# Regrouping the side work of a two-layer trunk: attention steps in groups, two transposed row tiles in one bank, state reads next to outer products

## The chip, the cores and the metric

The kernel runs on one core of a Trainium2 chip. The metric is the device time of one launch in microseconds; three runs are given for the kernel before, and their median is what a change is held against.

## The reference, cut to what matters

Two layers; each projects 512 tokens of 2048 features with one wide matrix, runs two kinds of heads on the result, and projects back. Around it stand RMS norms, SiLU gates and the residual sum.

```python
# softmax heads (8 of width 128): every frame sees its own chunk and the 8 before it
scores = einsum('bnqhd,bnkhd->bnhqk', qc, kb) * D ** -0.5 + bias
p = softmax(where(valid, scores, -inf)); o = einsum('bnhqk,bnkhd->bnqhd', p, vb)
# linear heads (4, keys 128, values 256), chunks of 64 frames
U = einsum('bnchk,bnchv->bnhkv', k * exp(L_end - L), v)      # outer products
state = exp(L_end) * state + U                               # one step per chunk
o = einsum('bnchk,bnhkv->bnchv', q * DK ** -0.5, states)     # reads
```

With 512 frames the band covers all earlier chunks, so each tile of 128 rows attends to the row tiles up to itself.

## The kernel before, in words

The bulk of the work is a list of large products: the projections, done as `std_gemm` (line 293) and, for the other pairs of column blocks, as `fast_gemm` (line 324), which forms seven products per pair out of sums of blocks. Each weight chunk is a Job: a load, a cast `wh` on ScalarE (line 201) and a remainder `wl` on VectorE (line 210), and then 12 matmuls of 512 columns (line 388), or 24 of 256 columns in the pairs that come out feature-major (line 378). A pair has 28 jobs. These matmuls take their operands as fp32r.

Everything else is side work. It is written as generators in `tasks` and is emitted between jobs: after each job `pace()` calls `pump(n)` (line 257), and each pump resumes the first generator of `tasks` up to its next `yield`. `delayed` holds calls that come due after so many pumps. `until` (line 272) pumps until a condition holds. The rate is 2.1 pumps a job in the pairs that hold the softmax heads, 2 in the pair that makes the linear heads' values (GV), and 3 in the pair after it (GG). This gives the program's order; the framework then simulates a timeline and lays out each engine's instructions by it, so that an instruction that is not ready in that simulation lets a later one go first, and the engines then run the order that came out.

Softmax attention: `attend` (line 988) runs two heads, a and b, through the hand-written list ORDER (line 983). `aS3` is the scores of row tile 3 of head a (`scores`, line 901: three fp32r matmuls, a DVE reduction at line 912, an exponential at 916). `aT3` transposes the probabilities of that tile (`trans`, line 924: i + 1 transposes of fp32 into one PSUM bank, then one copy out, by ScalarE for tiles 1 and 3 and by VectorE for 0 and 2). `aP3` multiplies them with the values (`mix`, line 935: i + 1 fp32 matmuls, each of which shows as two records, then a square on ScalarE). `aG` scales and gates the head (line 953), and eight pumps later `turn` (line 964) transposes its result. Each step ends in one `yield`, so a pair of heads takes 28 pumps.

Linear attention: `gla_heads` (line 1243) takes two heads in two halves each, four Units. `outer` (line 1089) forms a unit's chunk states' increments: 12 fp32r matmuls of 64 rows by 128 columns into two banks. `states` (line 1108) chains them on VectorE, four instructions. `read` (line 1124) multiplies queries with states: four fp32 matmuls of 128 rows by 64 columns, eight records. `norm` and `evict` follow on ScalarE, VectorE and GpSimd. Two of these generators run in each layer. A unit's reads are emitted six pumps after its states, five for the last unit; the outer product of unit k + 1 is emitted two pumps before the reads of unit k.

All side work takes its PSUM from one tag of four banks (`aux`, line 87).

Of the kernel before, what the change touches and what calls it, by code (L numbers as in the profile page):

```python
# [15 lines left out]
P = 128  # L16
L = 2
S = 512
# [15 lines left out]
def hybrid_trunk(  # L34
# [13 lines left out]
    nc = tc.nc  # L48
# [16 lines left out]
    def nm(s):  # L65
        serial[0] += 1
        return f"{s}_{serial[0]}"

    def slot(tag, shape, dtype=F32):
        return slots.tile([P] + shape, dtype, tag=tag, name=nm(tag))  # L70
# [4 lines left out]
    def t2(shape=(512,), dtype=F32):  # L75
        return tmp.tile([P] + list(shape), dtype, tag="t2", name=nm("t2"))
# [10 lines left out]
    def aux():  # L87
        return ps_ax.tile([P, 512], F32, tag="ax", name=nm("ax"))
# [12 lines left out]
    def flat(t):  # L101
        return t.bitcast(F32).rearrange("p a b -> p (a b)")

    def split(hi, lo, src):
        nc.scalar.copy(hi, src)
        return nc.vector.tensor_tensor(out=lo, in0=src, in1=hi.bitcast(F32), op=ALU.subtract).ins
# [9 lines left out]
    ident = cst[:, 0:P]  # L116
# [137 lines left out]
    delayed = []  # L254
# [356 lines left out]
    rows = []  # L611
# [117 lines left out]
    def layer(l):  # L729
# [163 lines left out]
        class Head:  # L893
# [28 lines left out]
                    load_bias(HEADS.index(self.hd) + 2)  # L922

            def trans(self, i):
                lk = (i + 1) * P
                ps = aux()
                for j in range(i + 1):
                    nc.tensor.transpose(ps[:, j * P : (j + 1) * P], self.prob[i][:, j * P : (j + 1) * P], ident)  # L928
                pt = self.pt[i] = t2((lk,))
                if i % 2:  # L930
                    nc.scalar.copy(pt, ps[:, :lk])
                else:
                    nc.vector.tensor_copy(pt, ps[:, :lk])
# [30 lines left out]
            def turn(self):  # L964
                c, kk = self.hd // 2, self.hd % 2
                if kk == 0:
                    turned[c] = slot("g16", [2, 512], F32R)
                ps = aux()
                for t in range(NT):
                    nc.tensor.transpose(ps[:, t * P : (t + 1) * P], self.sg[:, t, :], ident)  # L970
                kt = 8 + self.hd
                f = t2()
                nc.scalar.activation(
                    f, ps, AF.Copy, scale=gcol[:, l * 2 * KT + KT + kt : l * 2 * KT + KT + kt + 1]
                )
                last_turn[0] = nc.gpsimd.dma_start(of_att[l][c][:, kk, :], f).ins
                ks = slice(kk * 256, (kk + 1) * 256)
                z = turned[c]
                split(z[:, 0, ks], z[:, 1, ks], f[:, 0:256])
                if kk:  # L980
                    nc.gpsimd.dma_start(oa_d[l][c], flat(z))

        ORDER = (
            "aS3 aS2 aS1 aS0 aT3 bS3 aT2 aP3 bS2 aT1 aP2 bS1 aT0 aP1 bS0 aP0 - aG "
            "bT3 bT2 bP3 bT1 bP2 bT0 bP1 bP0 - bG"
        ).split()

        def attend(hd, qk):
            heads = {"a": Head(hd, qk, 0), "b": Head(hd + 1, qk, 1)}

            def turn(h):
                h.turn()
                if h.hd % 2:
                    heads_done.add(hd)

            for _ in range(5 if hd == HEADS[0] else 0):
                yield
            for step in ORDER:
                if step == "-":
                    yield  # L1000
                    continue
                h = heads[step[0]]
                if step[1] == "S":
                    h.scores(int(step[2]))
                elif step[1] == "T":
                    h.trans(int(step[2]))
                elif step[1] == "P":
                    h.mix(int(step[2]))
                else:
                    h.gate()  # L1010
                    delayed.append([8, lambda h=h: turn(h)])
                yield

        QKT = {(0, 1): ("g4", "g5", "g6", "g7"), (0, 0): ("g8", "g9", "g10", "g11"),
# [2 lines left out]
        def qk_consume(p):  # L1017
            sets = {}

            def f(j, h, b, src, comb):  # L1020
                if j not in sets:
                    if (p, j) == (1, 0):
                        until(lambda: 2 in heads_done)
                    sets[j] = [slot(tag, [2, 512], F32R) for tag in QKT[p, j]]
                z = settled(src, comb).rearrange("p (f n) -> p f n", f=2)
                hs = slice(h * 256, (h + 1) * 256)
                hi, lo = sets[j][2 * b][:, :, hs], sets[j][2 * b + 1][:, :, hs]
                if b == 0:
                    split_scaled(hi, lo, z, -QS)
                else:  # L1030
                    split(hi, lo, z)
                if h and b:
                    tasks.append(attend(4 * p + 2 * j, sets[j]))
            return f
# [38 lines left out]
        if last:  # L1073
            for t in range(2):
                rows = slice(t * P, (t + 1) * P)
# [167 lines left out]
        def gla_heads(j, gvh, gvl):  # L1243
            units = []

            def new(k):
                h, p = 2 * j + k // 2, k % 2
                units.append(Unit(h, p, gvh, gvl, units[-1] if p else None))
                units[-1].outer()

            for _ in range(4):
                yield
            new(0)
            yield
            units[0].states()
            yield
            for k in range(4):
                if k < 3:
                    new(k + 1)
                    yield  # L1260
                yield
                units[k].read()
                yield
                if k < 3:
                    units[k + 1].states()
                    yield
                units[k].norm()
                yield
                yield
                units[k].evict()  # L1270
                yield
            gla_done.update((2 * j, 2 * j + 1))

# [12 lines left out]
        def gv_consume(j, h, t, src, comb):  # L1286
            if (j, h) not in gvh:
                until(lambda: 4 in heads_done)
                gvh[j, h] = slot(GV[j][h], [2, 512], F32R)
                gvl[j, h] = slot(GV[j][2 + h], [2, 512], F32R)  # L1290
            split(gvh[j, h][:, t, :], gvl[j, h][:, t, :], settled(src, comb))
            if h and t:
                tasks.append(gla_heads(j, [gvh[j, p] for p in range(2)], [gvl[j, p] for p in range(2)]))
# [169 lines left out]
    for l in range(L):  # L1463
        layer(l)
# [54 lines left out]
```

## Time and profile before

| what | value |
|---|---|
| median of three runs | 1615.99 us (1614.28 to 1617.05) |
| span of the profiled execution | 1613.3 us |
| mean granted TensorE clock | 0.998 |
| softmax records: L945 (mix) | 320, 46.5 us busy |
| L928 (transposes) | 160, 27.5 us busy |
| linear heads: L1131 (reads) | 128, 20.3 us busy |
| L1103 (outer products) | 192, 15.6 us busy |

The page of the profile gives the span of one execution, from its first to its last instruction; it gives no other time of that execution, and the span lies 2.7 us under the median of the three runs. In rows of the timeline the columns are the start in us, the duration in us, the engine, the line of the kernel, the operation, the output and inputs, the shape and the count of merged instructions. Matmuls are pipelined, so the recorded duration of one reaches over the start of the next: what a matmul takes of the engine's time is read from one start to the next. "ax" is a bank of side work and "mm" one of the large products; "128*64" is rows by columns of the array that are used.

### The profile page before, as it was taken

The numbers are of one execution on the slowest core, as the hardware profiler recorded it, in microseconds if no ns is written. First come the engines' busy times: TensorE is split into PE (matmuls) and PEld (weight loads), VectorE is DVE, ScalarE is ACT, GpSimd is POOL, SyncE is SP. The second block draws the span as 40 slices with busy tenths as digits, with TensorE's granted clock in tenths as the row PEclk, the third lists the DMA queues.
The fourth block names the chain that finished last, engine by engine and source line by source line (L and its number), as shares of the span: only waits on it lengthen the run. The fifth ranks groups of instructions, "written<-read, shape, count | busy, mean of one in ns | idle before, by whom it ended". The sixth has DMA issues, their size and how long they took to land.

```text
span 1613.3 us, 24483 instructions
## 1 busy us (share of the span) xinstructions
PE 1600.6 (99%) x8938; PEld 1372.9 (85%) x8938; DVE 1271.7 (79%) x1646; ACT 919.5 (57%) x1509; POOL 127.5 (8%) x192
## 2 busy tenths in 40 slices
PE   9999999999999999999999999999999999999997
PEld 7888999998888778888888889999988887788886
DVE  5977777678677878998998677776786878689887
ACT  7544445657555546565796444455675545566654
POOL 0120000010000010100122000000100100101001
PEclk9999999999999999999999999999999999999999
DMA  9797686785868768689779786857858687686986
GB/s 371 258 371 271 238 304 206 230 308 168 286 213 282 261 221 313 227 309 377 270 267 369 312 312 222 306 193 260 299 198 292 209 301 254 221 307 228 342 302 190
DMA packets 133928, 438.17 MB, mean 272 GB/s; under 512 B 14404, under 2 KB 27204, under 8 KB 133776
## 3 DMA queue, kind: packets, MB, share of 16 engines
q1 hardware_dynamic: 117072, 375.99, 67.2%
q0 software_dynamic: 16160, 59.53, 10.0%
q8 instruction: 71, 1.16, 0.3%
q10 hardware_dynamic: 576, 1.08, 0.2%
q14 instruction: 49, 0.40, 0.1%
HBM read 377.02 MB, written 61.62 MB: 272 GB/s over the span
## 4 chain that ended last, share of the span: by engine, by line
PE 95%; DVE 2%; DMA 1%; ACT 1%; issue 1%; DVEq 0%; SPq 0%; ACTq 0%
PE mm L388 54%; PE mm L378 19%; PE mm L310 10%; PE ax L945 2%; PE ax L388 2%; PE ax L1131 1%; PE ax L928 1%; PE ax L752 1%; PE ax L1103 1%; PE ax L908 1%; PE ax L907 1%; PE ax L906 1%; DVE wl L210 1%; DMA bias<-in_rel_dram 0%; PE ax L1223 0%
## 5 line engine op out<-in xcount | busy, mean ns | idle before, releaser
L388 PE MATMUL mm<-wh,sa 128*128 128x512 f32 x1600 | 517.7, 394 | 0.6 <-ACT wh L201 0.5
L201 ACT CAST wh<-H 128x1024 fp32r<-128x1024 f32 x256 | 268.5, 1051 | 213.9 <-PE mm L388 94.0
L210 DVE TENSOR_TENSOR wl<-H,wh 128x1024 fp32r<-128x1024 f32 x256 | 311.6, 1219 | 94.3 <-PE mm L388 33.0
L388 PEld LDWEIGHTS mm<-wh,sa 128*128 128x128 f32 x1600 | 299.4, 188 | 72.8 <-issue 8.8
L201 ACT CAST wh<-raw 128x1024 fp32r<-128x1024 f32 (+1 forms) x233 | 244.0, 1051 | 197.1 <-PE mm L388 91.2
L210 DVE TENSOR_TENSOR wl<-raw,wh 128x1024 fp32r<-128x1024 f32 (+1 forms) x233 | 282.0, 1213 | 58.1 <-PE mm L388 25.7
L388 PE MATMUL mm<-wl,sa 128*128 128x512 f32 x800 | 312.6, 391 | 0.0
L378 PE MATMUL mm<-sa,wh 128*128 128x256 f32 x1280 | 237.4, 285 | 0.0
L388 PE MATMUL mm<-wh,a 128*128 128x512 f32 x640 | 211.5, 394 | 0.0
L378 PEld LDWEIGHTS mm<-sa,wh 128*128 128x128 f32 x1280 | 200.3, 191 | 0.3
L378 PE MATMUL mm<-sa,wl 128*128 128x256 f32 x640 | 180.9, 283 | 0.0
L388 PEld LDWEIGHTS mm<-wl,sa 128*128 128x128 f32 x800 | 150.3, 188 | 30.0 <-DVE wl L210 0.4
L195 DVE TENSOR_TENSOR H<-H,raw 128x1024 f32<-128x1024 f32 x144 | 174.6, 1217 | 1.0
L388 PEld LDWEIGHTS mm<-wh,a 128*128 128x128 f32 x640 | 119.5, 188 | 24.9
L388 PE MATMUL mm<-wl,a 128*128 128x512 f32 x320 | 125.6, 393 | 0.0
L378 PEld LDWEIGHTS mm<-sa,wl 128*128 128x128 f32 x640 | 122.5, 191 | 0.0
L430 POOL TENSOR_TENSOR sm<-sm,mhalf 128x2 f32<-128x2 f32 (+2 forms) x40 | 51.4, 1285 | 761.2 <-DVE sm L955 456.3
L197 DVE TENSOR_TENSOR raw<-H,raw 128x1024 f32<-128x1024 f32 x56 | 68.5, 1222 | 51.8 <-DMA raw<-in_w_dram 51.4
L388 PE MATMUL mm<-wh,g 128*128 128x512 f32 x320 | 101.5, 391 | 0.0
L378 PE MATMUL mm<-a,wh 128*128 128x256 f32 x512 | 95.4, 285 | 0.0
L340 ACT COPY ev<-mm 128x512 f32<-128x512 f32 x104 | 60.9, 585 | 60.5 <-PE mm L388 43.8
L216 DVE TENSOR_TENSOR H<-H,raw 128x1024 f32<-128x1024 f32 x48 | 58.7, 1223 | 35.3 <-DMA raw<-in_w_dram 35.0
(250 smaller groups left out, 2323.6 us busy)
## 6 DMA issues: line engine op xcount, KB each, us to landing
raw<-in_w_dram SPq DMA_DIRECT2D x311, 512.0 KB, 5.1
sa<-S SPq DMA_DIRECT2D x184, 512.0 KB, 4.5
H<-in_w_dram SPq DMA_DIRECT2D x64, 512.0 KB, 5.2
sa<-A SPq DMA_DIRECT2D x48, 512.0 KB, 5.8
S<-g POOLq DMA_DIRECT2D x32, 512.0 KB, 9.1
sa<-oS SPq DMA_DIRECT2D x32, 512.0 KB, 5.2
oS<-g POOLq DMA_DIRECT2D x16, 512.0 KB, 4.4
oS<-sa POOLq DMA_DIRECT2D x16, 512.0 KB, 5.7
```

Of the source, the lines that this page charges most:

```text
L195: nc.vector.tensor_tensor(out=h, in0=h, in1=r, op=ALU.add)
L197: nc.vector.tensor_tensor(out=r, in0=h, in1=r, op=ALU.subtract)
L201: last_cast[0] = nc.scalar.copy(self.wh[:, z, :], src[:, z, :]).ins
L210: last_low[0] = nc.vector.tensor_tensor(out=self.wl[:, z, :], in0=self.src[:, z, :], in1=self.wh[:, z, :].bitcast(F32), op=ALU.subtract).ins
L216: nc.vector.tensor_tensor(out=h, in0=h, in1=self.src, op=ALU.add)
L310: nc.tensor.matmul(pss[o], a(part, kk, o) if callable(a) else a[:, part, t], rhs[:, kk, :], start=(i == 0 and kk == 0 and m == 0), stop=(i ...
L340: last_copy[0] = nc.scalar.copy(e, src[t]).ins
L378: nc.tensor.matmul(dst, lhs[:, kk, f], a[:, part, tok], start=(fresh and kk == 0 and m == 0 and ft % 2 == 0), stop=(c == 3 and kk == 1 and ...
L388: last_mm[0] = nc.tensor.matmul(out_ps[t], a[:, part, tok], rhs[:, kk, :], start=(fresh and kk == 0 and m == 0), stop=(c == 3 and kk == 1 ...
L430: nc.gpsimd.tensor_tensor(out=out_r, in0=v, in1=mhalf[:, : v.shape[-1]], op=ALU.pow)
L752: nc.tensor.matmul(ps[0:96, half * 256 : (half + 1) * 256], wga[kt // 10][:, kt % 10, :], op[:, i, (kt % 2) * 256 : (kt % 2 + 1) * 256], s ...
L945: nc.tensor.matmul(o, self.pt[i][:, j * P : (j + 1) * P], av[hd // 4, j // 2][:, j % 2, (hd % 4) * P : (hd % 4 + 1) * P], start=(j == 0), ...
```

## The change

`ORDER` becomes a list of groups. All steps of a group are emitted in one pump, and each group is followed by two yields: 11 groups, 22 pumps for a pair of heads. A group that holds scores has them last, or first among the heads' steps of other kinds where it begins the list. Row tiles 1 and 0 are transposed by one call (`T1`) into one bank, side by side, and copied out by one VectorE instruction of 384 columns; only tile 3 is still copied by ScalarE. In `gla_heads` the reads of unit k and the outer product of unit k + 1 are emitted in the same pump, reads first; the states of unit k + 1 come two pumps after, and the reads of that unit five pumps after its states for every unit. A generator of linear heads takes 35 pumps in place of 32.

```diff
             def trans(self, i):
-                lk = (i + 1) * P
-                ps = aux()
-                for j in range(i + 1):
-                    nc.tensor.transpose(ps[:, j * P : (j + 1) * P], self.prob[i][:, j * P : (j + 1) * P], ident)
-                pt = self.pt[i] = t2((lk,))
-                if i % 2:
+                rows = (1, 0) if i == 1 else (i,)
+                lk = sum(z + 1 for z in rows) * P
+                ps, pt = aux(), t2((lk,))
+                o = 0
+                for z in rows:
+                    for j in range(z + 1):
+                        nc.tensor.transpose(
+                            ps[:, o + j * P : o + (j + 1) * P], self.prob[z][:, j * P : (j + 1) * P], ident
+                        )
+                    self.pt[z] = pt[:, o : o + (z + 1) * P]
+                    o += (z + 1) * P
+                if i == 3:
                     nc.scalar.copy(pt, ps[:, :lk])
                 else:
                     nc.vector.tensor_copy(pt, ps[:, :lk])
...
-        ORDER = (
-            "aS3 aS2 aS1 aS0 aT3 bS3 aT2 aP3 bS2 aT1 aP2 bS1 aT0 aP1 bS0 aP0 - aG "
-            "bT3 bT2 bP3 bT1 bP2 bT0 bP1 bP0 - bG"
-        ).split()
+        ORDER = tuple(
+            g.split() for g in (
+                "aS3", "aS2", "aS1 aS0", "aT3 aT2 bS3", "aP3 aP2 aT1 bS2", "aP1 aP0 bS1", "aG bS0",
+                "bT3 bT2", "bP3 bP2 bT1", "bP1 bP0", "bG",
+            )
+        )
...
-            for step in ORDER:
-                if step == "-":
-                    yield
-                    continue
-                h = heads[step[0]]
...
-                    delayed.append([8, lambda h=h: turn(h)])
+            for group in ORDER:
+                for step in group:
+                    h = heads[step[0]]
...
+                        delayed.append([8, lambda h=h: turn(h)])
+                yield
                 yield
...
             units[0].states()
             yield
+            yield
+            yield
             for k in range(4):
+                units[k].read()
                 if k < 3:
                     new(k + 1)
-                    yield
-                yield
-                units[k].read()
+                yield
                 yield
                 if k < 3:
                     units[k + 1].states()
...
                 units[k].evict()
+                yield
                 yield
```

More of the change, by code (lines that the diff above doesn't have):

```diff
@@ L997, in attend @@
                 yield
-            for step in ORDER:
-                if step == "-":
-                    yield
-                    continue
-                h = heads[step[0]]
[L1003 to L1010, printed above, removed]
-                    delayed.append([8, lambda h=h: turn(h)])
+            for group in ORDER:
+                for step in group:
+                    h = heads[step[0]]
+                    if step[1] == "S":
+                        h.scores(int(step[2]))
+                    elif step[1] == "T":
+                        h.trans(int(step[2]))
+                    elif step[1] == "P":
+                        h.mix(int(step[2]))
+                    else:
+                        h.gate()
+                        delayed.append([8, lambda h=h: turn(h)])
+                yield
                 yield
```

## The prediction

> **What bounds the kernel now.** I read the page first, then the waits of TensorE, then the chain that ended last, and then TensorE's own timeline around the side work.
>
> ```profile
> PE 1600.6 (99%) x8938; PEld 1372.9 (85%) x8938; DVE 1271.7 (79%) x1646; ACT 919.5 (57%) x1509; POOL 127.5 (8%) x192
> ```
> ```profile
> PE 95%; DVE 2%; DMA 1%; ACT 1%; issue 1%; DVEq 0%; SPq 0%; ACTq 0%
> ```
> ```profile
> PE ax L945 <- ACT t L931: 0.2, 1, 0.2
> ```
> ```profile
> 494.82 32.92 PE mm L388 x145
> ```
> ```profile
> 178.24 64.55 PE mm L378 x538
> ```
>
> TensorE is busy 99% of the span and is 95% of the chain. Its waits on the side work come to almost nothing: of all the attention's transposed tiles one was waited for, for 0.2 us. So an edit is worth what it takes out of TensorE's own stream of starts, and an earlier or later finish of VectorE or ScalarE is worth nothing as long as TensorE finds its operands. The last two rows, undisturbed runs of the chain, give the rulers: a 512-column matmul takes 32.92 / 145 = 0.227 us from start to start, a 256-column one 64.55 / 538 = 0.120 us. What a burst of side work costs is the distance across it less these.
>
> **Attention: the grouping and the joined bank.** The rows show three transposes alone, eight records of mixing alone, and the same two kinds in one burst.
>
> ```profile
> 326.60 0.49 PE L928 MATMUL ax<-cst,t 128*128 128x128 f32 x3
> 326.84 0.48 PE L378 MATMUL mm<-sa,wh 128*128 128x256 f32 x2
> 327.16 0.28 PE L378 MATMUL mm<-sa,wl 128*128 128x256 f32 x1
> ```
> ```profile
> 327.76 1.06 PE L945 MATMUL ax<-g,t 128*128 128x128 f32 x8
> 328.57 0.36 PE L378 MATMUL mm<-sa,wh 128*128 128x256 f32 x1
> 328.78 0.28 PE L378 MATMUL mm<-sa,wl 128*128 128x256 f32 x1
> ```
> ```profile
> 253.13 0.49 PE L928 MATMUL ax<-cst,t 128*128 128x128 f32 x3
> 253.46 1.06 PE L945 MATMUL ax<-g,t 128*128 128x128 f32 x8
> 254.27 0.48 PE L378 MATMUL mm<-a,wh 128*128 128x256 f32 x2
> 254.59 0.28 PE L378 MATMUL mm<-a,wl 128*128 128x256 f32 x1
> ```
>
> The trap is the duration column. The first large matmul behind a burst shows 0.48 or 0.36 where others of its kind show 0.28, which looks like a toll that grouping would save. From start to start there is none: alone, the transposes take 327.16 - 326.60 - 2 x 0.120 = 0.32 us and the mixing 328.78 - 327.76 - 0.120 = 0.90; together they take 254.59 - 253.13 - 2 x 0.120 = 1.22, the plain sum. The long first record only begins earlier, under the last transpose. All these are full-array shapes (128*128), before and after. So 11 groups in place of 28 steps, and where a burst ends, are worth nothing on TensorE; the transposes stay ten a head. I take -0.2 us for the one wait above. The mixing follows its transposes by one group, which mostly means a job between them, and that job, 24 x 0.120 = 2.9 us, hides the copy. At 2.1 pumps a job, one job in ten emits two groups at once, some eight times in the run, and there the cover is gone; each time would cost at most a copy, of these lengths:
>
> ```profile
> L933 DVE COPY t<-ax 128x384 f32<-128x384 f32 x16 | 8.8, 548 | 0.0
> L931 ACT COPY t<-ax 128x256 f32<-128x256 f32 x16 | 5.8, 363 | 1.4 <-PE ax L928 1.4
> L933 DVE COPY t<-ax 128x128 f32<-128x128 f32 x16 | 4.5, 282 | 0.0
> ```
>
> At 0.55 that end is +4.4 us; I take none of it, because a copy that the layout sees as late lets the next job's matmuls go first. The joined bank takes 363 + 282 ns in two copies away and adds one of 548 ns (the row of the same width), all of it on VectorE: 0.27 us more there for each of 16 heads, 4.3 us in the run, against 1613.3 - 1271.7 = 342 us in which VectorE is idle. What is queued behind the copy on VectorE is `wl` and the scores' reduction; nothing on TensorE has been late for those. A pair of heads ends six pumps sooner, so fewer pumps are forced where the next stage asks for finished heads; TensorE is full either way. I cost it at nothing.
>
> **Linear heads: reads beside outer products.** Here the shapes change: reads use 128*64 of the array, outer products 64*128, the large products 128*128.
>
> ```profile
> 533.90 0.39 PE L388 MATMUL mm<-wh,sa 128*128 128x512 f32 x1
> 534.22 0.98 PE L1103 MATMUL ax<-g,g 64*128 64x256 f32 x12
> 535.13 0.50 PE L388 MATMUL mm<-wh,a 128*128 128x512 f32 x1
> 535.47 0.40 PE L388 MATMUL mm<-wl,a 128*128 128x512 f32 x1
> ```
> ```profile
> 537.75 0.39 PE L388 MATMUL mm<-wh,a 128*128 128x512 f32 x1
> 538.07 1.08 PE L1131 MATMUL ax<-g,g 128*64 128x256 f32 x8
> 539.09 0.50 PE L388 MATMUL mm<-wh,sa 128*128 128x512 f32 x1
> 539.43 0.40 PE L388 MATMUL mm<-wl,sa 128*128 128x512 f32 x1
> ```
> ```profile
> 575.86 0.39 PE L388 MATMUL mm<-wh,sa 128*128 128x512 f32 x1
> 576.17 1.69 PE L1103 MATMUL ax<-g,g 64*128 64x256 f32 x24
> 577.79 0.50 PE L388 MATMUL mm<-wh,sa 128*128 128x512 f32 x1
> 578.13 0.40 PE L388 MATMUL mm<-wl,sa 128*128 128x512 f32 x1
> ```
> ```profile
> 587.13 0.39 PE L388 MATMUL mm<-wh,sa 128*128 128x512 f32 x1
> 587.45 0.97 PE L1103 MATMUL ax<-g,g 64*128 64x256 f32 x12
> 588.36 1.08 PE L1131 MATMUL ax<-g,g 128*64 128x256 f32 x8
> 589.37 0.50 PE L388 MATMUL mm<-wh,sa 128*128 128x512 f32 x1
> 589.70 0.39 PE L388 MATMUL mm<-wl,sa 128*128 128x512 f32 x1
> ```
>
> Each burst is entered late (0.32 us after the matmul before it, where 0.227 is usual) and left late (0.34 us between the two matmuls after it). Across, less two rulers of 0.227: outer products alone 535.47 - 533.90 - 0.454 = 1.116 us; reads alone 539.43 - 537.75 - 0.454 = 1.226; two outer products in a row 578.13 - 575.86 - 0.454 = 1.816; outer products followed by reads 589.70 - 587.13 - 0.454 = 2.116. So a pair of unlike bursts saves 1.116 + 1.226 - 2.116 = 0.226 us when joined, and two like ones save 2 x 1.116 - 1.816 = 0.416. The order of the change, reads first, does not occur before. Its bounds are these neighbours, 0.416 (no boundary left) and 0 (the boundary paid in full); I take 0.226, the row with the same two shapes.
>
> The Trainium skill, page "TensorEngine Tiling (Array Packing)", Key Properties, says that changing the tiling mode, not merely the tile, drains TensorE. Apart there are four such changes and joined three, and with 0.416 / 2 = 0.208 us a change a join would save 0.208 and ten joins 2.1 us in place of the 2.3 used below, an estimate from that page's rule; the trace agrees with the rule within that.
>
> Per layer the program joins six reads with outer products. Before, one such pair stands joined already (the last fence), so five are new: -1.13 us. The double outer product is lost, since those two are now four pumps apart: +0.42. That is -0.71 a layer, and -1.4 us in two layers, with ends of +0.8 (no saving) and -3.3 (0.416 each).
>
> The second term is bursts that come in pieces. The reads of a generator's last unit are cut before:
>
> ```profile
> 602.60 0.39 PE L388 MATMUL mm<-wh,sa 128*128 128x512 f32 x1
> 602.92 0.65 PE L1131 MATMUL ax<-g,g 128*64 128x256 f32 x2
> 603.50 0.50 PE L388 MATMUL mm<-wh,sa 128*128 128x512 f32 x1
> 603.83 0.39 PE L388 MATMUL mm<-wl,sa 128*128 128x512 f32 x1
> ```
> The last of its three pieces is the last burst of reads in that layer:
>
> ```profile
> 607.27 0.65 PE L1131 MATMUL ax<-g,g 128*64 128x256 f32 x2
> ```
>
> Such a piece of two records costs 603.83 - 602.60 - 0.454 = 0.776 us, nearly two thirds of a whole read. In the first layer ten bursts of reads stand alone between 538.07 and 607.27, for eight units of which one is in the joined burst: one unit lies in three pieces, one in two, and the first outer product in two. Put at the price of such a piece, three pieces cost 3 x 0.776 - 1.226 = 1.10 us too much, two 0.78, and the cut outer product the price of one burst's boundaries, 0.42: 2.30 a layer, 4.6 in all. These cuts come from the laid-out order: VectorE's four state steps stand between casts, and each read is placed as its state is ready. The last units keep their five pumps, so I expect these to stay mostly, and count a third gone, -1.5; the two middle units of each generator go from six pumps to five, eight in the run, and I count one newly cut, +0.8. The ends are -4.6 and +6.2 (all eight cut once).
>
> The linear generators take three pumps more each. By my count the pair after them has steps enough for all but a few, which are then run at once where the gates ask for finished heads; by then every read is out, and what is forced is ScalarE and VectorE work whose sum is not needed for three more jobs, 3 x 12 x 0.227 = 8 us. Without that cover it would cost up to a job, 2.7 us a layer; I cost it at nothing. PSUM stays within the four banks: a read's one and an outer product's two are live together, as before.
>
> **Sum.** -0.2 - 1.4 - 1.5 + 0.8 = -2.3 us on a span of 1613.3, giving 1611.0; the runs' median lies 2.7 us above the span, so the time is 1613.7 us.
>
> **The rivals.**
>
> *Everything whole.* Every burst is joined and none cut: -0.2 - 1.4 - 4.6 = -6.2, 1609.8 us. For it: most bursts before are whole, and with reads first a late state leaves the outer product to fill in. Against it: five pumps is the distance at which reads are cut today. Chance 0.20.
>
> *The reads do not land beside the outer products.* The layout by simulated readiness pulls them apart, so that the change does not do what it says. Then the joined pair and the double burst of before are lost too, 2 x (0.23 + 0.42) = +1.3, against -1.5 for pieces and -0.2: 1615.6 us, no change. For it: emission order is not the engines' order, as the pieces show. Against it: whole bursts stand where the program emits them, a job apart. Chance 0.22.
>
> *The middle reads come in pieces* (slower). The states now have five pumps before every read, in stages where VectorE is most wanted. With all eight newly cut in two, and the old pieces left: 8 x 0.78 - 1.4 - 0.2 = +4.6, 1620.6 us; in three pieces, 8 x 1.10 - 1.6 = +7.2, 1623.2. It decides from six of the eight on (6 x 0.78 - 1.6 = +3.1). For it: both cut units of before have exactly that distance. Against it: the first unit's reads, three pumps behind their states, are whole (the row at 538.07). Chance 0.12.
>
> My forecast has the remaining 0.46.
>
> **How the numbers follow.** A measurement can tell about 0.2%, 3.2 us, from no change; the three runs of before span 2.8. My forecast's own spread goes from 1611.3 (two thirds of the pieces gone, none new) to 1615.2 (none gone, one new); I let about 0.14 of its 0.46 pass the mark of 1612.8, and nearly all of the first rival: faster 0.34. Of the last rival 0.10 passes 1619.2: slower 0.10. The rest, 0.56, is the same. The range goes from 1609.6, just past "everything whole", to 1618.6, five of eight newly cut (5 x 0.78 - 1.6 = +2.3), or half of the attention's +4.4 on top of the forecast; outside lie most of the slower rival and a little below.
>
> **What would show it.** On TensorE's timeline reads (128*64) are directly followed by outer products (64*128), six times a layer, and such a burst takes 2.1 us less two rulers; a burst of transposes, mixing and scores costs the sum of its parts, with a long first record behind it. Bursts of reads in pieces are counted there too. I am wrong if attention's grouping changes TensorE's time by over 1 us, if a join of reads first saves nothing or far more than 0.23, if TensorE's waits on L931 or L933 grow to microseconds, or if the time moves without the count of bursts and pieces moving.

## The result, and the profile after

The changed kernel takes 1629.0 us (median of five, 1627.0 to 1630.9) against 1616.4 before: a ratio of 1.0076, 95% interval 1.0066 to 1.0087. It is 12.7 us slower, where the forecast was 2.3 us faster and the range ended at 1618.6.

The page of the profile after, its parts 1 and 4. The execution that was profiled is the slowest of the five, 1630.9 us with a span of 1629.2.

```profile
PE 1613.6 (99%) x8938; PEld 1377.0 (85%) x8938; DVE 1278.8 (78%) x1646; ACT 913.0 (56%) x1493; POOL 125.1 (8%) x192
...
PE 89%; DVE 4%; issue 3%; DMA 3%; ACT 1%; POOL 0%; DVEq 0%; SPq 0%; ACTq 0%; POOLq 0%
```

TensorE is as full as before, with the same 8938 matmuls, and yet is busy 13.0 us longer. The span of the profiled execution grew by 1629.2 - 1613.3 = 15.9 us, so only 2.9 of it is time in which TensorE was idle. That is the first sign that waiting is not the main cause: the same instructions took more of its time. The chain gives it 89% where it gave 95%, but a chain may run through a cast or a transfer while TensorE works beside it, so this share is no measure of a loss. Its waits say the same. All of them together come to 5.3 us in the profile after and to 2.3 in the one before. The three longest after:

```profile
PE ax L682 <- DVE t L679: 1.2, 1, 1.2
PE mm L388 <- DMA sa<-S: 1.1, 2, 0.7
PE ax L906 <- DVE t L939: 1.0, 1, 1.0
```

The first, at line 682, stands in the profile before with the same 1.2 us. The others are new: two waits on a transfer, and one of scores (L906) on the joined copy of probabilities in front of them (L939 is its new line), 2.1 us together. The groups of instructions name the place. From the profile before, reads and outer products:

```profile
L1131 PE MATMUL ax<-g,g 128*64 128x256 f32 x128 | 20.3, 394 | 0.0
...
L1103 PE MATMUL ax<-g,g 64*128 64x256 f32 x192 | 15.6, 294 | 0.0
```

And after, where the same code has lines 1138 and 1110, with attention's mixing (951) and transposes (931):

```profile
L951 PE MATMUL ax<-g,t 128*128 128x128 f32 x320 | 46.0, 274 | 0.0
L1138 PE MATMUL ax<-g,g 128*64 128x256 f32 x128 | 29.8, 401 | 0.0
L931 PE MATMUL ax<-cst,t 128*128 128x128 f32 x160 | 24.9, 272 | 0.0
L1110 PE MATMUL ax<-g,g 64*128 64x256 f32 x192 | 20.5, 305 | 0.0
```

As many reads and outer products as before fill 9.5 and 4.9 us more, while their mean records hardly lengthen. Busy time counts overlapping records once, so they overlap less. The single records of the trace show which overlap is gone: in a whole burst they start in pairs, 0.003 to 0.007 us apart, each using its half of the array, and in a cut one a record starts alone. TensorE's timeline shows how the bursts were cut. First a burst as the program means it, then one of the second half of the same layer:

```profile
538.34 0.39 PE L388 MATMUL mm<-wh,a 128*128 128x512 f32 x1
538.66 1.08 PE L1138 MATMUL ax<-g,g 128*64 128x256 f32 x8
539.67 0.98 PE L1110 MATMUL ax<-g,g 64*128 64x256 f32 x12
540.58 0.50 PE L388 MATMUL mm<-wh,sa 128*128 128x512 f32 x1
540.92 0.40 PE L388 MATMUL mm<-wl,sa 128*128 128x512 f32 x1
...
586.65 0.39 PE L388 MATMUL mm<-wh,sa 128*128 128x512 f32 x1
586.97 0.65 PE L1138 MATMUL ax<-g,g 128*64 128x256 f32 x2
587.55 0.38 PE L1110 MATMUL ax<-g,g 64*128 64x256 f32 x1
587.86 0.65 PE L1138 MATMUL ax<-g,g 128*64 128x256 f32 x2
588.43 0.38 PE L1110 MATMUL ax<-g,g 64*128 64x256 f32 x1
588.75 0.65 PE L1138 MATMUL ax<-g,g 128*64 128x256 f32 x2
589.32 0.38 PE L1110 MATMUL ax<-g,g 64*128 64x256 f32 x1
589.64 0.65 PE L1138 MATMUL ax<-g,g 128*64 128x256 f32 x2
590.21 0.85 PE L1110 MATMUL ax<-g,g 64*128 64x256 f32 x9
591.00 0.50 PE L388 MATMUL mm<-wh,sa 128*128 128x512 f32 x1
591.34 0.40 PE L388 MATMUL mm<-wl,sa 128*128 128x512 f32 x1
```

The first costs 540.92 - 538.34 - 0.454 = 2.126 us, a join of reads and outer products within 0.01 of the one before. The second holds the same eight records of reads and the same twelve of outer products, but they alternate, a single read (two records) and a single outer product, until the last nine outer products follow together, and it costs 591.34 - 586.65 - 0.454 = 4.236. Each turn of a read and an outer product takes 587.86 - 586.97 = 0.89 us. In the two layers together the reads lie in 42 pieces after (22 before, counted in the timeline as runs of reads with something else between) and the outer products in 30 (16 before).

Were the reads cut because their states came late? VectorE's timeline of the same unit says not:

```profile
582.14 0.42 DVE L1123 COPY g<-ax 128x256 f32<-128x256 f32 x1
582.66 1.51 DVE L1125 SCALAR_TENSOR_TENSOR g<-g,a_end,ax 128x256 f32<-128x256 f32 x3
```

All four states are done at 582.66 + 1.51 = 584.17, and the first of the alternating reads starts at 586.97, 2.8 us later. In the same way the states of all 16 units of that run were done before their first read started, by 1.6 us or more. The order of TensorE's instructions was laid out before the run, and on the chip the states did not ask for it.

### The profile page after: what moved, and what is told of

It reads as the page before. It is cut to its first block, busy times and chain, and to the rows that moved or that the text cites. A ratio compares the mean times of both kernels' runs of the same rounds, so it can differ in the third digit from the quotient of the medians.

```text
span 1629.2 us, 24414 instructions
## 1 busy us (share of the span) xinstructions
PE 1613.6 (99%) x8938; PEld 1377.0 (85%) x8938; DVE 1278.8 (78%) x1646; ACT 913.0 (56%) x1493; POOL 125.1 (8%) x192
## 4 chain that ended last, share of the span: by engine, by line
PE 89%; DVE 4%; issue 3%; DMA 3%; ACT 1%; POOL 0%; DVEq 0%; SPq 0%; ACTq 0%; POOLq 0%
PE mm L388 47%; PE mm L378 19%; PE mm L310 10%; PE ax L388 2%; PE ax L951 2%; PE ax L1138 2%; DVE wl L210 1%; DMA raw<-in_w_dram 1%; PE ax L1110 1%; PE ax L931 1%; PE ax L752 1%; DMA sa<-S 1%; PE ax L906 1%; PE ax L907 1%; PE ax L908 1%
## 5 line engine op out<-in xcount | busy, mean ns | idle before, releaser
L388 PE MATMUL mm<-wh,sa 128*128 128x512 f32 x1600 | 512.4, 393 | 1.4 <-DMA sa<-S 1.1
```

The source lines that it names most:

```text
L388: last_mm[0] = nc.tensor.matmul(out_ps[t], a[:, part, tok], rhs[:, kk, :], start=(fresh and kk == 0 and m == 0), stop=(c == 3 and kk == 1 ...
```

## The experiments

Theory 1: the loss is the reads in pieces. Its rivals: attention's grouping stalls TensorE, or holding reads until all states are there costs as much as the pieces. The first four runs put them apart. Ratios are to the kernel before, timed on the same chip.

**attn_only**: the changed attention (`ORDER`, `attend` and `trans` as in the change) with the linear heads of before, all their yields too.

```diff
-            yield
-            yield
             for k in range(4):
-                units[k].read()
                 if k < 3:
                     new(k + 1)
-                yield
+                    yield
+                yield
+                units[k].read()
                 yield
...
-                yield
                 yield
```

> Only the attention's part of the change: the grouped list and the joined bank; the linear heads' generator is that of the kernel before. Theory 1 (the loss lies in the linear heads' reads, which come in pieces): 1616 to 1619 us, no more than the 2.5 us that the second layer's attention lost in the profile after, and the reads' bursts as before. Rival 2 (the grouping stalls TensorE on copies and on late scores): most of the 12.7 us, 1626 to 1629.

Measured: 1616.6 us, ratio 1.0002 (0.9993 to 1.0011). Part 1 of its page:

```profile
PE 1600.7 (99%) x8938; PEld 1373.0 (85%) x8938; DVE 1277.7 (79%) x1646; ACT 911.7 (56%) x1493; POOL 128.7 (8%) x192
```

TensorE is busy 1600.7 us where it was 1600.6. The grouping, the bursts that end in scores and the joined bank gain or cost nothing that can be measured, which is to within some 1.5 us; rival 2 falls.

**gla_only**: the changed `gla_heads` in the kernel before, attention as it was.

> Only the linear heads' part: reads emitted with the outer products, attention as before. Theory 1: nearly the whole loss, 1626 to 1629 us, with the same 21 pieces of reads a layer as after. Rival 2: 1614 to 1618.

Measured: 1627.2 us, ratio 1.0070 (1.0057 to 1.0083). That is 10.7 us of loss where the whole change lost 12.7, and the two intervals overlap: nearly all of it comes from some moved yields and two statements. Its reads and outer products lie in the same 42 and 30 pieces.

**before_whole**: the kernel before with one edit, which makes a unit's reads one burst: the read of the last state is issued first, the others behind it.

```diff
-                for tt in range(2):
-                    for cc in range(2):
-                        q = 2 * tt + cc
-                        n = 4 * p + q
-                        nc.tensor.matmul(
+                first = None
+                for q in (3, 2, 1, 0):
+                    tt, cc = divmod(q, 2)
+                    n = 4 * p + q
+                    with tc.issue_after(first) if first is not None else nullcontext():
+                        ins = nc.tensor.matmul(
...
-                        )
+                        ).ins
+                    first = ins if first is None else first
+                    self.last_read = ins
```

> The kernel before, with only the reads held together (last state's read first); nothing joined, attention as before. Theory 1: the three pieces of one unit and the two of another become whole in each layer, 1.1 + 0.8 us, 3.8 us in two layers: 1612 to 1613 us. Rival 3: no gain or slower, with waits on the states.

Measured: 1611.7 us, ratio 0.9971 (0.9960 to 0.9983). The unit that lay in three pieces, in its timeline:

```profile
606.05 0.39 PE L388 MATMUL mm<-wh,sa 128*128 128x512 f32 x1
606.36 1.08 PE L1132 MATMUL ax<-g,g 128*64 128x256 f32 x8
607.38 0.50 PE L388 MATMUL mm<-wl,sa 128*128 128x512 f32 x1
607.72 0.40 PE L388 MATMUL mm<-wh,sa 128*128 128x512 f32 x1
```

It costs 607.72 - 606.05 - 0.454 = 1.216 us, a whole read, and no row of TensorE's waits in that run names the states: rival 3 falls too. Cuts of that sort were already in the kernel before, and taking them out is a gain of 4.8 us, a little more than expected.

**after_whole**: the changed kernel with the same edit, and the next outer products behind the last read.

```diff
-            def new(k):
+            def new(k, behind=None):
...
-                units[-1].outer()
+                with tc.issue_after(behind) if behind is not None else nullcontext():
+                    units[-1].outer()
...
-                    new(k + 1)
+                    new(k + 1, units[k].last_read)
```

> The changed kernel, with a unit's reads held together: the read of the last state is issued first and the three others behind it, and the next outer products behind the last read. So each unit's reads are one burst directly before 12 outer products. Theory 1: the pieces' price is gone and six joins a layer save 0.2 us each: about 5 us under before for the linear heads, plus 0 to 2.5 for attention, 1611 to 1614 us. Rival 2: the loss is elsewhere, 1622 us or more. Rival 3 (waiting for the last state stalls TensorE): 16 waits of up to 2 us, 1616 to 1630, with waits of TensorE on VectorE's states in the profile.

Measured: 1610.1 us, ratio 0.9965 (0.9953 to 0.9978). That is 1 us under its range. With the reads whole the change is 6 us under the kernel before; without that it is 13 over. The gain is the edit's more than the change's: the kernel before with that edit alone is 4.8 us faster, and the two intervals (0.9960 to 0.9983, and 0.9953 to 0.9978) overlap.

So the pieces are the cause of the loss. The second set asks why they came. Theory A is the one of the prediction's slower rival, five pumps from states to reads in place of six; theory B, that outer products emitted behind the reads no longer stand in front of them.

**after_far**: the changed kernel with two more yields behind `units[k + 1].states()`, so seven pumps.

> The changed kernel with two more yields between a unit's states and its reads (seven pumps in place of five, for every unit but the first of each generator). Theory A (the reads come in pieces because they stand five pumps behind their states): pieces go back to those of the kernel before or fewer, 1612 to 1618 us. Theory B (they come in pieces because no outer products stand in front of them any more: the layout comes to the reads while the states still come out one by one, and fills in between): still in pieces, 1622 to 1628.

Measured: 1624.5 us, ratio 1.0051 (1.0036 to 1.0066), with 36 pieces of reads and 34 of outer products. There are more pumps than before the change, and the reads are still in pieces: theory A falls. Distance in time may still play a part, for two units a layer that lay in three pieces in the changed kernel are whole here, while others are cut more.

**after_swap**: the changed kernel with two statements exchanged.

```diff
-                units[k].read()
                 if k < 3:
                     new(k + 1)
+                units[k].read()
```

> The changed kernel with two statements swapped: the outer products of the next unit first, then the reads, in the same pump; still five pumps from states to reads. Theory A: reads in pieces as after, about 1626 us. Theory B: the outer products stand in front, most reads are whole, each join saves the 0.2 us that outer products followed by reads saved before; with one unit a layer left in pieces 1614 to 1616 us.

Measured: 1616.5 us, ratio 1.0003 (0.9993 to 1.0012), 22 and 18 pieces. The pieces are as theory B had them, and the time is 0.5 us above its range, not below the kernel before. One unit a layer lies in four pieces: the last of the first generator, which has no outer products to be emitted in front of it. Its joined bursts look like this:

```profile
550.07 0.39 PE L388 MATMUL mm<-wh,sa 128*128 128x512 f32 x1
550.38 0.97 PE L1110 MATMUL ax<-g,g 64*128 64x256 f32 x12
551.28 1.08 PE L1138 MATMUL ax<-g,g 128*64 128x256 f32 x8
552.30 0.50 PE L388 MATMUL mm<-wh,sa 128*128 128x512 f32 x1
552.63 0.39 PE L388 MATMUL mm<-wl,sa 128*128 128x512 f32 x1
```

552.63 - 550.07 - 0.454 = 2.106 us. The program still emits six such pairs a layer, and five of them come out joined on the chip; all that was exchanged is which comes first.

**after_hold**: the changed kernel with the next outer products behind the last read, but the reads free to come one by one.

> The changed kernel with the next unit's outer products held behind the last of the reads, so that none can slip between two reads; the reads themselves are left to come as they are ready. If single outer products between the reads are what costs: 1616 to 1620 us. If each separate entry costs, whatever stands between (an entry behind one large matmul took 0.77 us in the profile of after, one behind a single outer product 0.89): still 1624 to 1629 us, with single large matmuls between the reads.

Measured: 1627.2 us, ratio 1.0071 (1.0056 to 1.0086). Its timeline at the unit shown above:

```profile
588.48 0.65 PE L1138 MATMUL ax<-g,g 128*64 128x256 f32 x2
589.05 0.49 PE L388 MATMUL mm<-wh,sa 128*128 128x512 f32 x1
589.48 0.65 PE L1138 MATMUL ax<-g,g 128*64 128x256 f32 x2
590.05 0.49 PE L388 MATMUL mm<-wl,sa 128*128 128x512 f32 x1
```

A large matmul has slipped in where the outer product was, and each turn takes 589.48 - 588.48 = 1.00 us, 0.77 of it not the large matmul's. So it is the separate entry that costs, whichever of these two stands between. It also suggests that the layout held the reads for something: with no outer product to fill in, it still placed other work after every read of this unit.

**gla_whole**: the linear heads of after_whole with the attention of before.

> The linear heads of the run with reads held together, with the attention of the kernel before. Theory 1: attention's grouping is worth nothing, so the time is that of the run with both, 1609 to 1612 us. If the grouping was worth what it is meant for, this is slower by as much: 1613 to 1616.

Measured: 1611.9 us, ratio 0.9971 (0.9961 to 0.9982), the time of after_whole within what can be told. It is also the time of before_whole (1611.7 us, the same ratio), which has no reads beside outer products but for one pair a layer: what the joins save does not show in the time of a launch. In the linear stretches of the table below it may: -2.9 and -3.8 us against -1.9 twice.

**whole_both** and **swap_whole_both**: reads whole and joined in either order, and the first outer product of a layer whole as well.

```diff
-                for tt in range(2):
+                for tt in (1, 0):
...
-                        ops.append(((kh, vh), (kh, vl), (kl, vh)))
+                        ops.append(((kh, vl), (kh, vh), (kl, vh)))
```

> The run with reads held together and joined, and also the first outer product made whole: its halves in the other order, and the product that is ready last put first. 16 bursts of reads, 16 of outer products, none cut. Against that run the two cut outer products save 0.4 us each: 0.8 us under it, 1609 to 1611 us; against the kernel before about 6 us, the sum of pieces (4.6) and joins (1.4). If it comes out at 1616, the price of pieces is wrong.

> The same, but with the outer products first and the reads directly behind them in each joined burst. A join of outer products followed by reads cost 2.116 us before and one of reads first 2.126 after, so the order inside a whole burst should not matter: the time of the run before it within 1 us, 1608 to 1612.

Measured: 1609.6 us, ratio 0.9958 (0.9945 to 0.9970), and 1610.4 us, ratio 0.9962 (0.9948 to 0.9975). Both beat both kernels: 6 to 7 us under the one before, 19 under the changed one. No read or outer product is cut in either, and which of the two comes first makes no difference that can be told, though the second has five joined pairs a layer on the chip where the first has six.

The runs in one table. "Linear stretches" are the profiled executions' time from the 2500th to the 3040th large matmul (lines 310, 378 and 388, counted from 0) and from the 6220th to the 6740th, less that of before: the part of each layer that holds these heads, free of what single executions do elsewhere. In brackets, waits of over 0.17 us between two large matmuls in it.

| kernel | us | pieces of reads, outer products | linear stretches, layer 1 and 2 |
|---|---|---|---|
| before | 1616.4 | 22, 16 | |
| changed | 1629.0 | 42, 30 | +6.7 (1.2), +6.1 (0.6) |
| gla_only | 1627.2 | 42, 30 | +5.8, +5.9 |
| after_hold | 1627.2 | 42, 18 | +4.6, +4.6 |
| after_far | 1624.5 | 36, 34 | +3.9, +3.0 |
| after_swap | 1616.5 | 22, 18 | +1.3 (1.7), -0.3 (0.7) |
| attn_only | 1616.6 | 22, 16 | -0.5, +0.3 (0.6) |
| before_whole | 1611.7 | 16, 16 | -1.9, -1.9 |
| gla_whole | 1611.9 | 16, 18 | -2.9, -3.8 |
| after_whole | 1610.1 | 16, 18 | -1.5 (1.5), -3.2 (0.7) |
| whole_both | 1609.6 | 16, 16 | -3.8, -4.6 |
| swap_whole_both | 1610.4 | 16, 16 | -1.8 (1.4), -3.5 |

The time follows the pieces of the reads. Small differences between the last five are not settled: waits of 1.5 us in one execution (after_whole, layer 1), most of it on a transfer, are as much as the joins are worth.

## Why the prediction was wrong, point by point

**Attention: right.** The term was -0.2 us, and attn_only measured no change. The reading that the long first record behind a burst is no toll, since the starts show the plain sum, holds. A term of -0.2 us is too small to be told in the time of a launch. The doubled groups left nothing that shows: no mixing waits for a copy in the profile after. Its one wait on a joined copy, 1.0 us, is of another kind, scores behind the transposes of their own group.

**The price of a join: right.** 0.226 us was taken from outer products followed by reads, with reads first unseen. Reads first cost 2.126 us, outer products first 2.106 to 2.116: the saving is the same. This is read from the timeline alone; in the time of a launch no run shows it apart (gla_whole against before_whole).

**The price of a cut: right where the trace had it.** The cuts of before were put at 1.10 and 0.78 us a layer, 1.88 together; before_whole took 1.9 us out of each layer's stretch.

**The number of cuts: this step failed.** The prediction said: "I count one newly cut", for +0.8 us, and counted a third of the old cuts gone, for -1.5. Reads went from 22 to 42 pieces and outer products from 16 to 30, and the two units a layer that were cut before are cut more, in three and four pieces where they lay in two and three. The size of the loss follows from that. By the prediction's own prices, 0.78 us for two pieces and 1.10 for three, and 4 x 0.77 - 1.226 = 1.85 for four (the turn of after_hold), a layer of the changed kernel, with one unit in two pieces, three in three and two in four, comes to 0.78 + 3.30 + 3.70 = 7.8 us too much, 5.9 more than the 1.88 before. This is an estimate that leaves out joins and cut outer products; the linear stretches measured 6.7 and 6.1.

Three things were wrong in that count. The reason that it gave, pumps between states and reads, is not enough to decide: seven pumps still left 36 pieces, and the old order of two statements brought 22 back. So the count, worked out from that reason, rested on nothing. The rows before had left two readings open: the last units, which were cut, stood five pumps behind their states, but they were also the only ones without outer products emitted in front of their reads. The first unit, whole at three pumps, had them in front, and spoke for the second reading. The bounds were too narrow: a cut was thought of as a piece set off by large matmuls, two or three a unit, for the middle units alone, while the reads of the second generator's first unit, with three pumps as before, came in four pieces too. And the prediction took the outer product that stands next to the reads as something to join; it did not see that what stands ready behind a read that is held back is also what gets placed between two reads, and that this cuts both kinds at once. The prediction has this even as a point in favour of its faster rival: "with reads first a late state leaves the outer product to fill in".

**The slower rival** had the mechanism, a chance of 0.12, and a price of 4.6 to 7.2 us; the measured loss is 12.7. It had the wrong trigger and too few pieces. One unit alone, in the timeline above, costs 4.236 - 2.126 = 2.1 us too much, twice what it allowed for a unit in three pieces.

**The upper end of the range**, 1618.6 us, follows from neither sum that was given for it: five of eight newly cut come to 1616.0 + 2.3 = 1618.3, and half of the attention's 4.4 on top of the forecast to 1613.7 + 2.2 = 1615.9. The result lies far beyond either.

**The forced pumps and the banks** were put at nothing, and no run speaks against it: after_whole has the same 35 pumps and is the faster.

What stays open is why the simulated timeline holds the reads apart when on the chip the states are long done. That it comes to the reads earlier, relative to VectorE, than the chip does is an inference: after_hold and after_swap fit it, but no run shows that timeline itself. The trace before fits it too: in the last unit of the first layer the states end at 596.60, 600.79 (the second of two) and 602.31, in steps of one, two and one, and the reads stand in pieces of one, two and one at 602.92, 605.09 and 607.27, each 4 to 6 us behind its state.

## What to carry to other kernels

When a tool lays out an engine's order, a change in the program is not yet a change in the order: count the bursts that come out, in the new order, before pricing them. Where a burst is dear to enter, tie its instructions together, the one whose input is ready last at the head, rather than moving them to where they ought to be ready; here that edit alone was worth 0.3%, and the changed kernel lost 0.8% without it and gained 0.4% with it. And an engine that is 99% busy, with waits of 5 us in all, can still lose 13 us: read what the same instructions take from start to start.

## What the runs showed of the hardware that had not been expected

A single read or outer product between others of another shape costs far more than its share of a burst. In the alternating unit of the changed kernel a read takes 587.55 - 586.97 = 0.58 us, where four take 539.67 - 538.66 = 1.01 in the whole burst, 0.25 each; an outer product takes 587.86 - 587.55 = 0.31, where twelve take 540.58 - 539.67 = 0.91, 0.08 each. That is over twice and some four times as much. The change of shape fits as the cause: bursts of transposes and mixing, which have the shape of the large products, cost the plain sum of their parts in the rows of the prediction, and the turn with a large matmul in the place of the outer product, also a change of shape, takes 0.77 us beside that matmul. The Trainium skill, page "TensorEngine Tiling (Array Packing)", Key Properties, says that changing the tiling mode drains TensorE; the trace agrees in that each change costs some 0.2 us (0.208 by the double burst of outer products, 0.22 to 0.24 by the joins), though it does not show that draining is what takes it. Where a read is left alone, the empty half of the array comes on top: its two records start one after the other, where in a burst another read's start beside them.
